# Two plain blocks of a convolutional feed-forward, emitted later behind the sums of h, and each block's taps emitted sequence by sequence

## The chip, the cores and the metric

One core of a Trainium2 chip runs the whole program in one launch. TensorE (PE) multiplies, VectorE (DVE), ScalarE (ACT) and GpSimd (POOL) do the elementwise work, SyncE (SP) issues most of the DMAs, and POOL issues the rest. The metric is the device time of one execution in microseconds (us); a number without a unit below is in us. Times inside an execution count from the start of its span.

## The reference, cut to what matters

Two sequences (256 and 512 tokens, model width 1024) go through two layers. Each layer is a mixer with four branches, which the change does not touch, and then a feed-forward with a depthwise convolution of three taps:

```python
def conv_ffn(h, w_up, w_dw, b_dw, w_down):
    u = depthwise_conv(h @ w_up, w_dw, b_dw)      # over time, per channel, each sequence alone
    a, b = jnp.split(u, 2, axis=-1)               # 2816 channels each
    return (jax.nn.silu(a) * b) @ w_down
...
x = x + conv_ffn(rms_norm(x, ffn_norm[l]), ffn_w_up[l], ffn_conv_w[l], ffn_conv_b[l], ffn_w_down[l])
```

## The kernel before

Both sequences stand side by side as 768 columns, the 512 first. Activations are kept with channels on the 128 partitions. To keep fp32 accuracy each matmul operand is split into a high part (a copy on ACT into fp32r) and a low part (the difference, on DVE), and each product is three matmuls: high x high, low x high, high x low. Weights arrive by DMA (`raw`), ACT makes `whi` (line 444), DVE makes `wlo` (line 453).

**The feed-forward in blocks.** 2816 channels are 22 blocks of 128, numbered 0 to 21. A block is two column groups of `w_up`: the gate half and the value half. Blocks 0 and 1 are *plain*: `ffn_plain` computes each half's 768 columns in two pieces of 384 (`plain_half`, copy out of PSUM by ACT in line 1475). Blocks 2 to 21 are done by `ffn_seven` with seven half-size products instead of eight, in Strassen's manner. For these, sums and differences of the quarters of h are needed. `t_gen` makes them on DVE (lines 640 to 652) with their splits (lines 626 and 628), and `t3_gen` splits one more quarter. The products of a seven-product block stand on PE in this order: `X` (the quarter b11), T1, *T4 of the block before* (`ffn_rest`), T2 (adds into X), b21, b22 and T3 (adds into X again). Each is 12 matmuls of 128x384. ACT copies X after the first product (line 1532), which T2 waits for, because T2 overwrites that PSUM tile. DVE subtracts X after T3 (line 1547), which T4 waits for in the same way. On weights the same scheme needs sums of `raw` tiles, made by DVE (line 435, called `sum`) or by a DMA that accumulates.

**A block's tail** follows its products and is written as generators, resumed at times of the program's own clock:

- for each half `ffn_u`: the middle tap and the bias on ACT (line 1461), then `ffn_conv`, the two outer taps for the 512 columns (lines 1455 and 1457, 128x511) and for the 256 (the same lines, 128x255). All four are DVE operations with both tensors in SBUF
- `ffn_glu`: tanh on ACT (line 1569), a multiply-add on DVE (line 1571), a product of the two halves on POOL (line 1572), the high part on ACT (line 1574), the low part on DVE (line 1576)

After blocks 2 to 4 comes a *down step*, the product of blocks 0 to 3 with `w_down`, into the PSUM tiles `mm`; then blocks 5 to 8 and the down step of 4 to 7, and so on (`FF_SEQ`). So a down step needs the low part of the block that was finished last but one. Its matmuls take the blocks in order, so that part is needed for the fourth block of four.

**What sets the order.** Nothing is scheduled by a tool: every engine runs its instructions in the order in which this program emits them. The program keeps a clock (`self.now`) that advances with each emitted matmul by an estimate of its length. A generator in `self.fast` is resumed when the clock has passed its time; the number that it yields is the delay until the next resumption. `go_fast(gen, delay)` starts one. Weight splits are emitted by `pump` at the same points. So a delay decides only behind which other instructions an operation stands on its engine; the waits themselves are semaphores.

The change touches `ffn_u` (line 1464), which all 22 blocks use, and the two `go_fast` calls of `ffn_plain` (lines 1497 and 1501).

Of the kernel before, what the change touches and what calls it, by code (L numbers as in the profile page):

```python
# [19 lines left out]
NS, NP = 512, 256  # L20
NT = NS + NP
# [226 lines left out]
class Net:  # L248
# [1215 lines left out]
    def ffn_u(self, u, z, col):  # L1464

        self.ffn_mid(u, z, col)
        yield 1.3
        for c0, c1 in ((0, NS), (NS, NT)):
            self.ffn_conv(u, z[:, c0:c1], col, c0, c1)

    def plain_half(self, z, c0, w, rel=0):

# [4 lines left out]
    def ffn_plain(self):  # L1477

        cols = [c + j for j in range(FF_PLAIN) for c in (0, NFF)]
        n = 3  # L1480
        wts = [self.units(2, 128) for _ in cols]
        zs = [self.b() for _ in cols]
        self.finish(0)
        for w, z in zip(wts[:n], zs):
            self.plain_half(z, 0, w)
        self.finish(HALF)
        e = [self.now, self.t_gen()]
        self.fast.append(e)
        for w, z in zip(wts[:n], zs):
            self.plain_half(z, HALF, w, 4)  # L1490
        for w, z in zip(wts[n:], zs[n:]):
            self.plain_half(z, HALF, w)
            if w is wts[-1]:
                self.run_out(e)
                e = [self.now, self.t3_gen()]
                self.fast.append(e)
                self.go_fast(self.ffn_block(0, *zs[0:2]), 1.0)
            self.plain_half(z, 0, w, 4)
        self.run_out(e)
        for j in range(1, FF_PLAIN):  # L1500
            self.go_fast(self.ffn_block(j, *zs[2 * j:2 * j + 2]), 12.0 * j)

    def y(self):
        return self.pm.tile([128, NT], F32, tag="y", name=self.nm("y"), bufs=3)
# [274 lines left out]
```

## Time and profile before

| | |
|---|---|
| runs | 2726.26, 2729.82, 2730.07; median 2729.82 |
| the profiled execution | 2730.13, its span 2728.4 |
| mean granted TensorE clock | 0.989 of full speed |
| PE busy | 2677.2 (98% of the span) |
| DVE busy | 1729.2 (63%) |
| ACT busy | 1141.3 (42%) |
| POOL busy | 634.0 (23%) |
| share of the chain that ended last | PE 86%, DVE 8%, ACT 2%, POOL 1%, DMA 1% |

The profile is of one execution. Busy shares are means over the whole span, and the four engines stand idle at different places. The stretch that the change touches is the feed-forward of each layer. In layer 0 its tails begin at about 880, and five of its down steps begin between 932 and 1314. In layer 1 the same rows come 1358.9 later. A wait is attributed to the semaphore that came last.

### The profile page before, as it was taken

The numbers are of one execution on the slowest core, as the hardware profiler recorded it, in microseconds if no ns is written. First come the engines' busy times: TensorE is split into PE (matmuls) and PEld (weight loads), VectorE is DVE, ScalarE is ACT, GpSimd is POOL, SyncE is SP. The second block draws the span as 40 slices with busy tenths as digits, with TensorE's granted clock in tenths as the row PEclk, the third lists the DMA queues.
The fourth block names the chain that finished last, engine by engine and source line by source line (L and its number), as shares of the span: only waits on it lengthen the run. The fifth ranks groups of instructions, "written<-read, shape, count | busy, mean of one in ns | idle before, by whom it ended". The sixth has DMA issues, their size and how long they took to land.

```text
span 2728.4 us, 40139 instructions
## 1 busy us (share of the span) xinstructions
PE 2677.2 (98%) x15196; PEld 2439.2 (89%) x15196; DVE 1729.2 (63%) x3048; ACT 1141.3 (42%) x2333; POOL 634.0 (23%) x592
## 2 busy tenths in 40 slices
PE   9999999999998999999999999999999989999999
PEld 8779998888898899999987799988888989999998
DVE  6644448887437866686746454478873388766875
ACT  6443443223224554554544434432232255544553
POOL 3402123122222212222314021131121212222221
PEclk9999999999999999999999999999999999999999
DMA  5101113212232466646731111131212325567556
GB/s 167 43 28 37 41 56 114 63 62 62 62 129 81 107 148 128 155 121 147 193 94 43 28 40 48 51 114 63 66 59 62 132 74 127 137 130 161 125 136 163
DMA packets 143264, 258.87 MB, mean 95 GB/s; under 512 B 20192, under 2 KB 36192, under 8 KB 143072
## 3 DMA queue, kind: packets, MB, share of 16 engines
q1 hardware_dynamic: 118368, 197.59, 22.7%
q0 software_dynamic: 24704, 58.73, 12.4%
q8 instruction: 119, 1.95, 0.3%
q14 instruction: 73, 0.60, 0.1%
HBM read 205.78 MB, written 48.91 MB: 93 GB/s over the span
## 4 chain that ended last, share of the span: by engine, by line
PE 86%; DVE 8%; issue 2%; ACT 2%; POOL 1%; DMA 1%; SPq 0%; DVEq 0%; ACTq 0%; POOLq 0%
PE mm L498 35%; PE ps L498 26%; PE mm L522 16%; PE ps L511 3%; DVE wlo L453 2%; PE ps L904 1%; PE ps L1137 1%; PE ps L937 1%; PE ps L1088 1%; DMA raw<-wu 1%; PE ps L1140 1%; POOL st L529 1%; DVE b L612 1%; DVE hl L628 0%; PE ps L851 0%
## 5 line engine op out<-in xcount | busy, mean ns | idle before, releaser
L453 DVE TENSOR_TENSOR wlo<-raw,whi 128x512 fp32r<-128x512 f32 (+1 forms) x616 | 480.8, 790 | 142.3 <-ACT whi L444 117.9
L498 PE MATMUL ps<-b,whi 128*128 128x384 f32 (+2 forms) x1888 | 466.2, 340 | 17.3 <-ACT s L1532 11.7
L444 ACT CAST whi<-raw 128x512 fp32r<-128x512 f32 (+1 forms) x616 | 370.0, 614 | 237.2 <-PE ps L498 72.3
L498 PEld LDWEIGHTS ps<-b,whi 128*128 128x128 f32 x1888 | 329.7, 191 | 34.4 <-ACT s L1532 12.3
L498 PE MATMUL mm<-b,whi 128*128 128x512 f32 (+1 forms) x1504 | 322.9, 336 | 0.6 <-DVE b L1576 0.6
L522 PE MATMUL mm<-whi,hh 128*128 128x512 f32 (+2 forms) x752 | 308.8, 411 | 7.5 <-ACT hh L547 5.7
L498 PE MATMUL mm<-hh,whi 128*128 128x512 f32 (+1 forms) x1152 | 302.1, 343 | 0.0
L498 PE MATMUL ps<-b,wlo 128*128 128x384 f32 (+2 forms) x944 | 299.1, 339 | 0.0
L498 PE MATMUL mm<-hh,wlo 128*128 128x512 f32 (+1 forms) x1152 | 296.8, 338 | 0.0
L498 PE MATMUL mm<-hl,whi 128*128 128x512 f32 (+1 forms) x1152 | 294.7, 337 | 0.0
L522 PE MATMUL mm<-whi,hl 128*128 128x512 f32 (+2 forms) x752 | 278.8, 371 | 0.8 <-DVE hl L554 0.8
L522 PE MATMUL mm<-wlo,hh 128*128 128x512 f32 (+2 forms) x752 | 278.5, 370 | 0.0
L498 PE MATMUL ps<-hh,whi 128*128 128x384 f32 x768 | 259.6, 338 | 8.5 <-ACT whi L444 8.5
L498 PEld LDWEIGHTS mm<-b,whi 128*128 128x128 f32 x1504 | 237.0, 188 | 26.6 <-DVE b L1576 1.2
L498 PE MATMUL ps<-hl,whi 128*128 128x384 f32 x768 | 259.4, 338 | 1.2 <-DVE hl L628 1.2
L498 PE MATMUL ps<-hh,wlo 128*128 128x384 f32 x768 | 258.2, 336 | 0.0
L529 POOL TENSOR_TENSOR st<-st,mhalf 128x16 f32<-128x16 f32 (+5 forms) x50 | 95.0, 1900 | 573.6 <-DVE st L1012 355.7
L1368 POOL TENSOR_TENSOR b<-b,b 128x768 f32<-128x768 f32 x48 | 100.2, 2087 | 463.4 <-DVE b L1363 463.4
L498 PEld LDWEIGHTS mm<-hh,whi 128*128 128x128 f32 x1152 | 177.3, 189 | 26.6 <-issue 3.1
L522 PEld LDWEIGHTS mm<-whi,hh 128*128 128x128 f32 x752 | 177.6, 236 | 25.6 <-issue 10.2
L498 PEld LDWEIGHTS mm<-hl,whi 128*128 128x128 f32 x1152 | 175.7, 188 | 25.1
L498 PEld LDWEIGHTS mm<-hh,wlo 128*128 128x128 f32 x1152 | 176.0, 188 | 24.4
(233 smaller groups left out, 4607.9 us busy)
## 6 DMA issues: line engine op xcount, KB each, us to landing
raw<-wu SPq DMA_DIRECT2D x600, 256.0 KB, 2.7
xsp<-y POOLq DMA_DIRECT2D x66, 384.0 KB, 5.8
raw<-wu POOLq DMA_DIRECT2D x80, 256.0 KB, 4.9
b<-xsp SPq DMA_DIRECT2D x24, 384.0 KB, 6.8
xsp<-b POOLq DMA_DIRECT2D x22, 384.0 KB, 5.7
do<-ot SPq DMA_DIRECT2D x36, 132.0 KB, 1.8
b<-do SPq DMA_DIRECT2D x12, 384.0 KB, 3.5
raw<-wu SPq DMA_DIRECT2D x16, 208.0 KB, 3.6
```

The costliest lines, as they stand in the source:

```text
L444: self.nc.scalar.copy(hi, raw)
L453: self.nc.vector.tensor_sub(lo, raw, hi.bitcast(F32))
L498: nc.tensor.matmul(ap, w, x[:, c0:c1], start=(k == 0 and i == 0 and not more), stop=(k == K - 1 and i == 2), skip_group_check=more)
L511: self.nc.tensor.transpose(out, x, self.ident)
L522: nc.tensor.matmul(ap, x[:, cols], w, start=(k == 0 and i == 0), stop=(k == 7 and i == 2))
L529: self.nc.gpsimd.tensor_tensor(r, ms, self.mhalf[:, 0:n], op=ALU.pow)
L612: nc.vector.scalar_tensor_tensor(h, h, g[:, k:k + 1], self.rbc[:, cols], op0=ALU.mult, op1=ALU.mult)
L904: nc.tensor.matmul(sc[:, 0:S], qkT[hh][:, 128 * t:128 * t + 128], qkT[4 + hh][:, 128 * t0:128 * t0 + S], start=True, stop=True)
L937: nc.tensor.matmul(sh["po"][:, hh, :], PT[:, 128 * kb:128 * kb + 128], v[(t0 + kb) // 3][:, (t0 + kb) % 3, 64 * hh:64 * hh + 64], start=(k ...
L1088: nc.tensor.matmul(sc[:, x, y, 0:W], qT[y][rr, 128 * t:128 * t + 128], kT[y][rr, k0:k0 + W], start=True, stop=True)
L1137: nc.tensor.matmul(po[:, 0, 2 * y + par, :], PT[0:c - a, 2 * z + y, :], vv[:, hc], start=(z == 0), stop=(z == 1))
L1368: nc.gpsimd.tensor_add(a, a, t)
```

## The change

The first conv half of each block now yields 0.9 between the taps of the 512 columns and those of the 256. The tail of block 0 starts 9.0 after the last plain product's first piece instead of 1.0, and that of block 1 starts 18.0 after the plain products instead of 12.0.

```diff
--- before.py
+++ after.py
@@ -1465,8 +1465,9 @@
 
         self.ffn_mid(u, z, col)
         yield 1.3
-        for c0, c1 in ((0, NS), (NS, NT)):
-            self.ffn_conv(u, z[:, c0:c1], col, c0, c1)
+        self.ffn_conv(u, z[:, 0:NS], col, 0, NS)
+        yield 0.9
+        self.ffn_conv(u, z[:, NS:NT], col, NS, NT)
 
     def plain_half(self, z, c0, w, rel=0):
 
@@ -1494,11 +1495,11 @@
                 self.run_out(e)
                 e = [self.now, self.t3_gen()]
                 self.fast.append(e)
-                self.go_fast(self.ffn_block(0, *zs[0:2]), 1.0)
+                self.go_fast(self.ffn_block(0, *zs[0:2]), 9.0)
             self.plain_half(z, 0, w, 4)
         self.run_out(e)
         for j in range(1, FF_PLAIN):
-            self.go_fast(self.ffn_block(j, *zs[2 * j:2 * j + 2]), 12.0 * j)
+            self.go_fast(self.ffn_block(j, *zs[2 * j:2 * j + 2]), 18.0 * j)
 
     def y(self):
         return self.pm.tile([128, NT], F32, tag="y", name=self.nm("y"), bufs=3)
```

All lines from 1469 on move down by one, so line 1532 of before is 1533 of the changed kernel, 1547 is 1548, 1571 is 1572 and 1576 is 1577. The same instructions are emitted on every engine, 3048 on DVE in both; PE's matmuls keep their order. What moves is the order on DVE, ACT and POOL, and with it some DMA issues. Three places on DVE follow (tiles are named by the program; the last number of a name is the program's running number, which shifts between the two).

Place 1 is DVE at the end of the sums of h in layer 0, before. `hl` are low parts of h, `y_..._8231` is the first half of plain block 0, and `sum_..._8275` is a weight sum of block 3:

```order
L628 TENSOR_TENSOR hl_1342_7261<-b_1355_7276,hh_1341_7260 128x384
L1455 SCALAR_TENSOR_TENSOR y_1490_8231<-b_1440_7890,fc_1_80,y_1490_8231 128x511
L1457 SCALAR_TENSOR_TENSOR y_1490_8231<-b_1440_7890,fc_1_80,y_1490_8231 128x511
L1455 SCALAR_TENSOR_TENSOR y_1490_8231<-b_1440_7890,fc_1_80,y_1490_8231 128x255
L1457 SCALAR_TENSOR_TENSOR y_1490_8231<-b_1440_7890,fc_1_80,y_1490_8231 128x255
L453 TENSOR_TENSOR wlo_1492_8252<-raw_1475_8132,whi_1491_8236 128x512
L628 TENSOR_TENSOR hl_1344_7263<-b_1356_7278,hh_1343_7262 128x384
L453 TENSOR_TENSOR wlo_1497_8273<-raw_1437_7866,whi_1493_8261 128x512
L435 TENSOR_TENSOR sum_1498_8275<-raw_1475_8132,raw_1474_8130 128x512
```

and with the change (`y_..._8311` is that half of block 0, `sum_..._8269` that weight sum):

```order
L628 TENSOR_TENSOR hl_1342_7261<-b_1355_7276,hh_1341_7260 128x384
L453 TENSOR_TENSOR wlo_1491_8246<-raw_1475_8132,whi_1490_8234 128x512
L628 TENSOR_TENSOR hl_1344_7263<-b_1356_7278,hh_1343_7262 128x384
L453 TENSOR_TENSOR wlo_1496_8267<-raw_1437_7866,whi_1492_8255 128x512
L435 TENSOR_TENSOR sum_1497_8269<-raw_1475_8132,raw_1474_8130 128x512
L453 TENSOR_TENSOR wlo_1500_8287<-sum_1497_8269,whi_1498_8277 128x512
L435 TENSOR_TENSOR sum_1501_8289<-sum_1497_8269,raw_1476_8134 128x512
L453 TENSOR_TENSOR wlo_1503_8306<-raw_1476_8134,whi_1502_8297 128x512
L453 TENSOR_TENSOR wlo_1507_8326<-sum_1501_8289,whi_1505_8316 128x512
L1455 SCALAR_TENSOR_TENSOR y_1504_8311<-b_1440_7890,fc_1_80,y_1504_8311 128x511
```

The four taps of block 0 stood ahead of two weight splits, a split of h and the weight sum; now they stand behind these and four more weight operations. Their two sequences still follow each other directly.

Place 2 is DVE ahead of the subtraction that T4 of block 3 waits for, before (`s_..._8265` is block 2, `s_..._8399` block 3's value half):

```order
L1571 SCALAR_TENSOR_TENSOR s_1495_8265<-s_1495_8265,s_1520_8397 128x768
L453 TENSOR_TENSOR wlo_1548_8544<-raw_1515_8364,whi_1547_8534 128x512
L1544 TENSOR_TENSOR s_1521_8398<-s_1521_8398,ps_1527_8430 128x384
L453 TENSOR_TENSOR wlo_1551_8557<-raw_1519_8394,whi_1549_8546 128x512
L1547 TENSOR_TENSOR s_1522_8399<-s_1522_8399,ps_1523_8400 128x384
```

and with the change:

```order
L1572 SCALAR_TENSOR_TENSOR s_1494_8259<-s_1494_8259,s_1518_8388 128x768
L453 TENSOR_TENSOR wlo_1549_8548<-raw_1517_8383,whi_1546_8533 128x512
L1455 SCALAR_TENSOR_TENSOR y_1548_8537<-b_1443_7893,fc_1_80,y_1548_8537 128x511
L1457 SCALAR_TENSOR_TENSOR y_1548_8537<-b_1443_7893,fc_1_80,y_1548_8537 128x511
L1455 SCALAR_TENSOR_TENSOR y_1548_8537<-b_1443_7893,fc_1_80,y_1548_8537 128x255
L1457 SCALAR_TENSOR_TENSOR y_1548_8537<-b_1443_7893,fc_1_80,y_1548_8537 128x255
L1548 TENSOR_TENSOR s_1520_8390<-s_1520_8390,ps_1521_8391 128x384
```

The four taps of block 1's second half now stand between block 2's multiply-add and the subtraction; of the two splits and the addition that stood there, one split is left.

Place 3 is DVE ahead of the low part of block 7 (line 1576), which the second down step takes as its last operand, before (`s_..._9479` and `s_..._9480` are block 8):

```order
L1571 SCALAR_TENSOR_TENSOR s_1686_9324<-s_1686_9324,s_1713_9478 128x768
L1544 TENSOR_TENSOR s_1714_9479<-s_1714_9479,ps_1722_9512 128x384
L453 TENSOR_TENSOR wlo_1741_9625<-raw_1710_9458,whi_1740_9615 128x512
L1547 TENSOR_TENSOR s_1715_9480<-s_1715_9480,ps_1716_9481 128x384
L453 TENSOR_TENSOR wlo_1746_9646<-raw_1726_9538,whi_1743_9635 128x512
L1576 SCALAR_TENSOR_TENSOR b_1737_9594<-s_1686_9324,b_1736_9593 128x768
```

and with the change:

```order
L1545 TENSOR_TENSOR s_1714_9479<-s_1714_9479,ps_1722_9509 128x384
L1572 SCALAR_TENSOR_TENSOR s_1686_9324<-s_1686_9324,s_1713_9478 128x768
L453 TENSOR_TENSOR wlo_1741_9625<-raw_1710_9456,whi_1740_9613 128x512
L1548 TENSOR_TENSOR s_1715_9480<-s_1715_9480,ps_1716_9481 128x384
L453 TENSOR_TENSOR wlo_1746_9646<-raw_1726_9538,whi_1743_9635 128x512
L1455 SCALAR_TENSOR_TENSOR s_1744_9638<-s_1714_9479,fc_1_80,s_1744_9638 128x511
L1457 SCALAR_TENSOR_TENSOR s_1744_9638<-s_1714_9479,fc_1_80,s_1744_9638 128x511
L1577 SCALAR_TENSOR_TENSOR b_1739_9605<-s_1686_9324,b_1738_9604 128x768
```

The pair of 128x511 taps of block 8's first half moved ahead of block 7's low part, and the addition of line 1544 (now 1545) ahead of its multiply-add. The same difference stands at the low parts of blocks 11 and 15 and, of block 3, at the first down step. Layer 1 repeats all three places. On ACT, the middle tap of line 1461 for block 8 likewise moved ahead of block 7's high part.

## Rows read from the trace of the kernel before

**Rows 1.** The page, engines' busy time, share of span, instructions.

```profile
PE 2677.2 (98%) x15196; PEld 2439.2 (89%) x15196; DVE 1729.2 (63%) x3048; ACT 1141.3 (42%) x2333; POOL 634.0 (23%) x592
```

**Rows 2.** Waits of PE in the whole span: waiter, awaited, total us, times, longest.

```profile
PE ps L498 <- ACT s L1532: 11.7, 2, 5.9
...
PE ps L498 <- DVE s L1547: 5.4, 3, 2.5
```

**Rows 3.** Timeline of PE, 880 to 938: start, us, instruction, idle before and releaser.

```profile
888.34 1.01 PE L498 MATMUL ps<-b,whi 128*128 128x384 f32 x2 [5.84 <-ACT s L1532]
...
920.08 1.01 PE L498 MATMUL ps<-b,whi 128*128 128x384 f32 x2 [2.49 <-DVE s L1547]
...
935.90 0.62 PE L498 MATMUL mm<-b,whi 128*128 128x512 f32 x2 [0.21 <-DVE b L1576]
```

**Rows 4.** Stretches: length, PE, PEld, DVE, ACT, POOL busy, granted clock, DMA.

```profile
888.00:892.30 4.30, 3.96 (x12) 3.96 (x13) 4.26 (x8) 2.66 (x5) 0.00 (x0) 0.50 0.01 4
...
920.20:924.00 3.80, 3.80 (x14) 3.80 (x15) 3.76 (x6) 2.63 (x6) 0.00 (x0) 0.59 0.42 138
```

**Rows 5.** Timeline of ACT around the first wait, 880 to 888.

```profile
880.02 1.03 ACT L1461 ACTIVATE y<-b,fc 128x768 f32<-128x768 f32 x1
...
887.29 0.62 ACT L444 CAST whi<-sum 128x512 fp32r<-128x512 f32 x1 [3.08 <-DVE sum L435]
887.81 0.47 ACT L1532 COPY s<-ps 128x384 f32<-128x384 f32 x1
```

**Rows 6.** Timeline of DVE, 882 to 935.

```profile
882.00 0.56 DVE L628 TENSOR_TENSOR hl<-b,hh 128x384 fp32r<-128x384 f32 x1 [1.23 <-ACT hh L626]
882.48 0.75 DVE L1455 SCALAR_TENSOR_TENSOR y<-b,fc,y 128x511 f32<-128x511 f32 x1
...
883.93 0.48 DVE L1455 SCALAR_TENSOR_TENSOR y<-b,fc,y 128x255 f32<-128x255 f32 x1
...
884.84 0.68 DVE L453 TENSOR_TENSOR wlo<-raw,whi 128x512 fp32r<-128x512 f32 x1
...
886.52 0.68 DVE L435 TENSOR_TENSOR sum<-raw,raw 128x512 f32<-128x512 f32 x1
...
919.49 0.54 DVE L1547 TENSOR_TENSOR s<-s,ps 128x384 f32<-128x384 f32 x1
...
934.90 0.95 DVE L1576 SCALAR_TENSOR_TENSOR b<-s,b 128x768 fp32r<-128x768 f32 x1
```

**Rows 7.** Timeline of POOL, two products of block tails.

```profile
913.48 1.85 POOL L1572 TENSOR_TENSOR b<-b,y 128x768 f32<-128x768 f32 x1 [14.91 <-DVE b L1571]
916.82 2.19 POOL L1572 TENSOR_TENSOR s<-s,s 128x768 f32<-128x768 f32 x1 [1.50 <-DVE s L1571]
```

**Rows 8.** Timeline of POOL and DVE in the mixer, around 534.

```profile
534.09 2.16 POOL L1368 TENSOR_TENSOR b<-b,b 128x768 f32<-128x768 f32 x1 [8.11 <-DVE b L1363]
...
534.47 2.73 DVE L1241 SCALAR_TENSOR_TENSOR b<-b,mc,b 128x508 f32<-128x508 f32 x2
```

**Rows 9.** Timeline of DVE ahead of the second down step.

```profile
1021.95 0.95 DVE L1571 SCALAR_TENSOR_TENSOR s<-s,s 128x768 f32<-128x768 f32 x1
...
1023.28 2.15 DVE L453 TENSOR_TENSOR wlo<-raw,whi 128x512 fp32r<-128x512 f32 x1
...
1025.82 0.68 DVE L453 TENSOR_TENSOR wlo<-raw,whi 128x512 fp32r<-128x512 f32 x1
1026.43 0.95 DVE L1576 SCALAR_TENSOR_TENSOR b<-s,b 128x768 fp32r<-128x768 f32 x1
```

**Rows 10.** Timeline of ACT there: the high part of block 7.

```profile
1024.92 0.85 ACT L1574 ACTIVATE b<-s 128x768 fp32r<-128x768 f32 x1 [0.20 <-POOL s L1572]
```

**Rows 11.** Timeline of PE in that down step: its fourth block.

```profile
1027.19 0.86 PE L498 MATMUL mm<-b,whi 128*128 128x512 f32 x4
```

**Rows 12.** Timeline of PE in layer 1's mixer: an idle time.

```profile
1478.26 0.32 PE L511 MATMUL ps<-hc,b 128*96 128x128 f32 x1 [1.63 <-DVE b L762]
```

**Rows 13.** The stretch behind that idle time, columns as in rows 4.

```profile
1478.30:1482.00 3.70, 3.70 (x21) 3.07 (x22) 2.95 (x7) 2.00 (x5) 0.21 (x1) 1.00 0.00 0
```

## The prediction

> **What bounds the kernel now.** I read the page's engine table first, then the list of what PE waits for, then PE's own timeline at the three longest of these waits in the feed-forward, the granted clock of the stretch behind them, and last the timelines of the engine that PE was waiting for. PE is busy for 98% of the span [rows 1]. A change that moves no matmul can therefore act only through the little that PE waits, or through waits that it makes. The waits for ACT's copy of X add up to 11.7 in two occurrences, and those for line 1547 to 5.4 [rows 2]. Both come once per layer: 5.84 at 888.34, ahead of T2 of block 2, and 2.49 at 920.08, ahead of T4 of block 3 [rows 3]. A third, 0.21 at 935.90, is the first down step waiting for the low part of block 3.
>
> Behind the two longer waits the granted clock reads 0.50 and 0.59 [rows 4]. Twelve matmuls took 4.00 there instead of 2.08, so the first wait costs 1.92 more than itself. The second stretch costs (1 - 0.59) x 3.80 = 1.58 more.
>
> The chain of the first wait can be read backwards. PE waits for the copy that ACT starts at 887.81; the copy stood on ACT behind `whi<-sum`, which waited 3.08 for DVE's weight sum [rows 5]. DVE started that sum at 886.52, and from 882.48 to 884.84, 2.36 long, it had done the four taps of block 0 [rows 6]. These taps are what the change takes from that place.
>
> From the same rows come the prices that I use, as the time from one start to the next on a DVE that doesn't wait. A 384-column operation is 0.47 (882.00 to 882.48), four taps are 2.36, and the pair of 128x511 taps alone is 1.45 (882.48 to 883.93) [rows 6]. A weight split or sum is 0.60 (1025.82 to 1026.43), and a multiply-add or low part is 0.87, the 1.33 from 1021.95 to 1023.28 less 0.47 [rows 9].
>
> **The change part by part.** *The first wait gets shorter.* Block 0's middle tap, at 880.02 on ACT, costs ACT 0.9 [rows 5] ahead of the split of h that DVE waits 1.23 for [rows 6]. With the change it stands behind, so DVE starts that split at 881.10. Then come 0.47 + 0.60 + 0.47 + 0.60, and the sum starts at 883.24. From sum to `whi` took 0.77, to the copy 0.52, to PE 0.53. T2 starts at 885.06 instead of 888.34: the wait falls from 5.84 to 2.6, and 3.3 are won. The wait that is left is as long as the one of 2.49, so I leave it a clock cost of 1.58, and 0.3 more are won.
>
> *Then DVE is late for T4.* What has moved back still stands ahead of the subtraction of block 3. Before, from 882.00 to the end of that subtraction, 919.95, there are 37.95. Of these 32.2 are work: 18 splits and sums x 0.60, 8 x 0.47, 6 sets of taps x 2.36 and 4 x 0.87. The other 5.75 are waits. With the change the work is 31.3, as one 0.87 of block 1 falls behind the subtraction. If the waits stay at 5.75, the subtraction ends at 881.10 + 31.3 + 5.75 = 918.2. But I replayed the new order with these prices, and waits come in: DVE has caught up with ACT and PE, and waits for two copies of sums (0.8 and 0.9) and for two products of PE (0.7 and 1.0). It waits about 1.8 for ACT elsewhere. Two holds of about 1.4 come on top, which the next paragraph prices. These overlap what was waited for before in part, and the replay gives 7.8 to 8.4 in all, an end at 920.3 to 920.9. PE arrives 3.6 earlier than before, at 914.0, and waits to about 920.5. What the first wait gave is gone.
>
> *The holds.* A weight split that DVE begins inside a POOL product takes 2.15 instead of 0.68 [rows 9]. In the feed-forward of before no tap begins inside such a product, so nothing there shows whether taps are held too. In the mixer two taps that began 0.4 inside a product took 2.73 together [rows 8], some 1.3 more than the like pair of 1.45. With the change the taps of block 1's second half begin inside the product of block 1 or 2 (the tail's parts move, and these taps now stand ahead of T4's subtraction), so I charge 1.2 to 1.5. A product is 1.85 to 2.19 long [rows 7]. The Trainium skill, "SBUF — State Buffer", section "Who interferes with whom", has a rule for this: a DVE instruction with two SBUF inputs contends with a GpSimd instruction that reads SBUF, and whichever was issued first keeps the shared port for its whole length. The rows in the mixer agree, and by the rule moved taps would be held wherever they meet a product; without it the sum below would be some 1.5 less per layer, 2749 in all.
>
> *The first down step is late.* From the end of T4's subtraction to the start of block 3's low part there were 14.95 [rows 6], of which 13.54 are work. Now there are 15.86: the 0.87 of block 1 and the pair of taps of 1.45 that moved ahead of the low part come in. The wait of 1.42 in it grows to between 3.5 and 4.2, since block 1's high part, waiting for POOL, stands ahead of a middle tap on ACT, and two more holds come in. Then the low part ends at 920.3 + 15.86 + 3.5 + 0.95 = 940.6 at the least, and at 920.9 + 15.86 + 4.2 + 0.95 = 941.9 at the most, instead of 935.85: 4.8 to 6.0 later. I take 6.0, since the products there follow a DVE subtraction as the one of 2.19 does [rows 7]. The lower bound, no wait beyond those of before, is 918.2 + 15.86 + 1.42 + 0.95 = 936.4, or 0.5 later. PE's new wait of about 5 lies between the two that cost clock: 1.6, with bounds 0 and 1.92.
>
> *The later down steps.* At the second one the low part of block 7 starts at 1026.43 and so ends at 1027.38 [rows 9]. PE needs it for the third matmul of the group of four that starts at 1027.19 [rows 11], half of 0.7 in, at 1027.54. The slack is under 0.2. With the change the addition of 0.47 stands ahead of the multiply-add, so the product, which ended just before 1024.92 [rows 10], ends at 1025.4 to 1025.8. The split held by it ends 0.6 later, the pair of taps takes 1.45 and the low part 0.95, which gives 1028.4 to 1028.8. PE waits 0.9 to 1.3, and I take 1.1. The bounds are 0.5, if nothing is held, and 1.75, if 0.47 and 1.45 are simply added to 1027.38. Blocks 11 and 15 have the same order. Of the clock I charge nothing here: after an idle time of 1.63 in layer 1's mixer [rows 12] the granted clock still read 1.00 [rows 13].
>
> *All else.* The other moved rows (the 0.9 between the taps of every other half, the moved DMA issues) I cost at nothing, since PE waits for none of their results and DVE stands idle for 37% of the span; without that cover a set of taps would cost its 2.36.
>
> The sum per layer is 6.0 + 1.6 + 3 x 1.1 = 10.9. The shorter first wait is no term of its own, as PE meets DVE again at T4. Two layers give 21.8. The profiled execution took 2730.13, 0.3 above the median of the runs, so the forecast is **2752**.
>
> **The rivals.** *Faster (chance 0.13).* The first wait shrinks by 3.3 and T4's wait goes with its slow clock. That is 3.3 + 0.3 + 2.49 + 1.58 = 7.7 per layer, and the time is 2715. It decides by whether the subtraction of block 3 ends by 914.0; my replay has it 6 later, the most lenient sum 4 later. For it speaks only that the two longest waits stand exactly there and that DVE idles much on the mean.
>
> *No change (0.12), 2730.* The first wait shrinks, T4 gives it back, and the low parts stay within half a microsecond of now because ACT and POOL run ahead of my replay. A change that doesn't do what it says would land here too, but the order shows its rows moved. Against it stands the slack of under 0.2.
>
> *Only the later down steps are late (0.15).* The first down step absorbs its delay, as in the lower bound, and only the 3 x 1.1 per layer stay: 2736.7.
>
> *Forecast case (0.60).* All three: from 2 x (0.5 + 0 + 1.5) = 4 more, 2734, to 2 x (6.0 + 1.92 + 5.25) = 26 more, 2757.
>
> **How the numbers follow.** A measurement of this kernel can tell some 0.2%, or 5.5, from no change. Slower by more than that hold the forecast case and the third rival, 0.60 + 0.15 = 0.75; within it the second, 0.12; faster the first, 0.13. The range reaches from the rival of no change, 2729, to the top of the forecast case, 2757, and leaves out the faster case. The forecast case's own range is 2734 to 2757.
>
> **What would show it.** In the changed profile the wait ahead of T2 of block 2 should be about 2.6, T4 of block 3 should still wait until about 920.5, and the first down step should wait some 5 for line 1577, with a granted clock of 0.5 to 0.6 behind it. Waits for that line should come eight times in all, six of them of about 1.1. Sets of taps that begin inside a product should read longer than 1.45 a pair. I am wrong if T4 starts before 916, if the low part of block 3 ends before 937, or if the later down steps run without a wait.

## The result and the profile after

| | before | changed |
|---|---|---|
| median of 4 runs each | 2729.57 | 2750.22 |
| lowest and highest | 2726.26, 2730.07 | 2749.23, 2754.10 |
| the profiled execution | 2730.13, span 2728.4 | 2754.10, span 2752.3 |
| mean granted clock | 0.989 | 0.987 |

The changed kernel is slower: the ratio estimated over the runs is 1.0084, with a 95% interval from 1.0071 to 1.0097 (the two medians alone give 1.0076). The forecast was 2752. The profiled execution is the slowest of the four; its parts therefore add up to somewhat more than the medians' difference of 20.7.

The page's engine table of the changed kernel, columns as in [rows 1]:

```profile
PE 2684.6 (98%) x15196; PEld 2443.3 (89%) x15196; DVE 1728.3 (63%) x3048; ACT 1136.7 (41%) x2333; POOL 641.0 (23%) x592
```

DVE has as much work as before. PE has 7.4 more, for the same 15196 matmuls; the stretches with a granted clock of 0.50 and 0.55 below show where it is slower. The waits of PE, with columns as in [rows 2]:

```profile
PE ps L498 <- DVE s L1548: 10.3, 2, 5.1
PE mm L498 <- DVE b L1577: 10.0, 8, 1.4
...
PE ps L498 <- ACT s L1533: 5.2, 2, 2.6
PE mm L498 <- ACT b L1575: 5.1, 2, 2.6
```

The wait for the copy of X is down from 11.7 to 5.2 in the two layers. In its place stand 10.3 for the subtraction of line 1548, 10.0 in eight waits for low parts (line 1577) and 5.1 for high parts (line 1575). PE's timeline shows where they are in layer 0 (against [rows 3]):

```profile
885.74 0.61 PE L498 MATMUL ps<-b,whi 128*128 128x384 f32 x2 [2.58 <-ACT s L1533]
...
909.15 0.45 PE L498 MATMUL ps<-hh,whi 128*128 128x384 f32 x1 [0.74 <-ACT s L1539]
...
914.25 0.61 PE L498 MATMUL ps<-b,whi 128*128 128x384 f32 x2 [0.66 <-DVE s L1542]
...
921.76 1.01 PE L498 MATMUL ps<-b,whi 128*128 128x384 f32 x2 [5.13 <-DVE s L1548]
...
940.66 0.64 PE L498 MATMUL mm<-b,whi 128*128 128x512 f32 x2 [2.49 <-ACT b L1575]
...
942.65 1.01 PE L498 MATMUL mm<-b,whi 128*128 128x512 f32 x2 [1.36 <-DVE b L1577]
...
1038.69 0.62 PE L498 MATMUL mm<-b,whi 128*128 128x512 f32 x2 [1.23 <-DVE b L1577]
```

T2 of block 2 starts at 885.74 after 2.58, T4 of block 3 at 921.76 after 5.13. Then the first down step waits twice, 2.49 for the high part of block 3 and 1.36 for its low part, and the second one waits 1.23. The granted clock behind the waits at T4, at the first down step and at the second one (columns as in [rows 4]):

```profile
921.70:926.50 4.80, 4.74 (x15) 4.74 (x16) 4.73 (x9) 2.48 (x5) 0.00 (x0) 0.50 0.17 55
940.60:945.50 4.90, 3.48 (x11) 2.95 (x12) 4.74 (x8) 1.32 (x3) 0.06 (x1) 0.55 0.34 54
1038.60:1041.00 2.40, 2.31 (x13) 2.22 (x14) 2.27 (x6) 0.80 (x1) 0.19 (x1) 1.00 0.37 69
```

It reads 0.50, 0.55 and 1.00. DVE ahead of T4 and of the low part of block 3 (against [rows 6]), and the two POOL products that the first two of its rows meet:

```profile
902.22 2.33 DVE L435 TENSOR_TENSOR sum<-raw,raw 128x512 f32<-128x512 f32 x1
...
917.25 2.29 DVE L1455 SCALAR_TENSOR_TENSOR y<-b,fc,y 128x511 f32<-128x511 f32 x1
...
921.16 0.55 DVE L1548 TENSOR_TENSOR s<-s,ps 128x384 f32<-128x384 f32 x1
...
931.14 0.75 DVE L1455 SCALAR_TENSOR_TENSOR s<-s,fc,s 128x511 f32<-128x511 f32 x1 [1.28 <-ACT s L1461]
...
941.65 0.95 DVE L1577 SCALAR_TENSOR_TENSOR b<-s,b 128x768 fp32r<-128x768 f32 x1
```

```profile
901.85 2.15 POOL L1573 TENSOR_TENSOR b<-b,y 128x768 f32<-128x768 f32 x1 [5.38 <-DVE b L1572]
...
916.81 2.18 POOL L1573 TENSOR_TENSOR s<-s,s 128x768 f32<-128x768 f32 x1 [12.81 <-DVE s L1572]
```

The sum at 902.22 began inside the product of 901.85 and took 2.33 instead of 0.68; the first tap of block 1's second half began inside the product of 916.81 and took 2.29 instead of 0.75 [rows 6]. The subtraction that T4 waits for could start only at 921.16. At 931.14 stands the wait of 1.28 for the middle tap on ACT, and the low part of block 3 starts at 941.65 instead of 934.90. Ahead of the second down step (against [rows 9]):

```profile
1034.02 0.55 DVE L1548 TENSOR_TENSOR s<-s,ps 128x384 f32<-128x384 f32 x1
...
1034.49 1.82 DVE L453 TENSOR_TENSOR wlo<-raw,whi 128x512 fp32r<-128x512 f32 x1
...
1036.24 0.74 DVE L1455 SCALAR_TENSOR_TENSOR s<-s,fc,s 128x511 f32<-128x511 f32 x1
...
1037.01 0.75 DVE L1457 SCALAR_TENSOR_TENSOR s<-s,fc,s 128x511 f32<-128x511 f32 x1
...
1037.68 0.95 DVE L1577 SCALAR_TENSOR_TENSOR b<-s,b 128x768 fp32r<-128x768 f32 x1
```

```profile
1033.62 2.16 POOL L1573 TENSOR_TENSOR s<-s,s 128x768 f32<-128x768 f32 x1 [1.93 <-DVE s L1572]
```

The split that began inside the product took 1.82 (the subtraction ahead of it, which reads PSUM, only 0.55), the pair of taps follows, and the low part of block 7 stands behind both.

Since PE runs the same matmuls in the same order, the start of one matmul can be compared in the two traces. The difference tells what each place cost (changed minus before):

| matmul | before | changed | difference |
|---|---|---|---|
| last one ahead of T2 of block 2 | 882.15 | 882.83 | 0.67 |
| first of T2 of block 2 | 888.34 | 885.74 | -2.60 |
| first of T4 of block 3 | 920.08 | 921.76 | 1.68 |
| first down step, low part of block 3 | 935.90 | 942.65 | 6.75 |
| last ahead of block 7's low part | 1027.42 | 1037.17 | 9.75 |
| on block 7's low part | 1027.54 | 1038.69 | 11.15 |
| on block 11's low part | 1119.06 | 1131.76 | 12.70 |
| on block 15's low part | 1210.60 | 1224.79 | 14.19 |
| end of the feed-forward of layer 0 | 1329.63 | 1343.26 | 13.63 |

From 0.67 to 13.63 is 12.96 for layer 0. Layer 1's feed-forward goes from 10.51 to 23.97, 13.46. Between the two feed-forwards, where the change does nothing, the difference falls from 13.63 to 10.51. In layer 1's mixer, from 2028 to 2140 alone, it falls by 1.9, with a granted clock of 1.00 in both executions. I take no account of that, and below I compare kernels by these sums over the two feed-forwards, beside their times.

### The profile page after: what moved, and what is told of

Read it like the earlier page. It is cut to its first block, busy times and chain, and to the rows that moved or that the text cites. A ratio compares the mean times of both kernels' runs of the same rounds, so it can differ in the third digit from the quotient of the medians.

```text
span 2752.3 us, 40171 instructions
## 1 busy us (share of the span) xinstructions
PE 2684.6 (98%) x15196; PEld 2443.3 (89%) x15196; DVE 1728.3 (63%) x3048; ACT 1136.7 (41%) x2333; POOL 641.0 (23%) x592
## 4 chain that ended last, share of the span: by engine, by line
PE 84%; DVE 9%; issue 2%; ACT 2%; POOL 1%; DMA 1%; SPq 0%; ACTq 0%; DVEq 0%; POOLq 0%
PE mm L498 34%; PE ps L498 26%; PE mm L522 15%; PE ps L511 3%; DVE wlo L453 3%; PE ps L904 1%; PE ps L1137 1%; PE ps L1088 1%; PE ps L937 1%; DVE s L1455 1%; PE ps L1140 1%; DVE b L1577 1%; POOL st L529 1%; DVE b L612 1%; PE ps L851 0%
## 5 line engine op out<-in xcount | busy, mean ns | idle before, releaser
L453 DVE TENSOR_TENSOR wlo<-raw,whi 128x512 fp32r<-128x512 f32 (+1 forms) x616 | 474.6, 777 | 153.5 <-ACT whi L444 123.3
L498 PE MATMUL ps<-b,whi 128*128 128x384 f32 (+2 forms) x1888 | 469.9, 342 | 16.8 <-DVE s L1548 10.3
L498 PEld LDWEIGHTS ps<-b,whi 128*128 128x128 f32 x1888 | 332.2, 192 | 34.2 <-DVE s L1548 10.9
```

What stands on the lines that cost most here:

```text
L453: self.nc.vector.tensor_sub(lo, raw, hi.bitcast(F32))
L498: nc.tensor.matmul(ap, w, x[:, c0:c1], start=(k == 0 and i == 0 and not more), stop=(k == K - 1 and i == 2), skip_group_check=more)
```

## The experiments

All kernels were timed against the kernel before, each group beside runs of its own of it, whose medians lie between 2727.4 and 2729.6; the ratios carry 95% intervals. "Feed-forwards" is the sum described above, from the profiled executions, for layer 0 and layer 1.

| kernel | median | ratio | feed-forwards |
|---|---|---|---|
| changed | 2750.22 | 1.0084 [1.0071, 1.0097] | 13.0, 13.5 |
| the 0.9 alone | 2746.79 | 1.0075 [1.0060, 1.0090] | 8.3, 11.0 |
| both delays alone | 2733.45 | 1.0025 [1.0015, 1.0034] | 2.6, 3.7 |
| block 0's delay alone | 2733.01 | 1.0020 [1.0009, 1.0031] | 1.1, 2.5 |
| block 1's delay alone | 2735.73 | 1.0033 [1.0021, 1.0046] | 2.6, 5.1 |
| taps apart, tail on time | 2740.26 | 1.0048 [1.0033, 1.0063] | 4.9, 7.4 |
| taps together, tail late | 2762.43 | 1.0127 [1.0112, 1.0142] | 16.2, 17.5 |
| down step behind block 5 | 2730.24 | 1.0013 [1.0004, 1.0023] | |
| that, with 9.0 and 24.0 | 2729.57 | 1.0008 [0.9998, 1.0018] | |
| changed, products on DVE | 2744.39 | 1.0055 [1.0040, 1.0070] | 8.5, 8.6 |
| before, products on DVE | 2724.82 | 0.9988 [0.9979, 0.9998] | |
| block 0's delay, products on DVE | 2726.13 | 0.9990 [0.9981, 1.0000] | |
| down step behind block 5, 9.0 and 24.0, products on DVE | 2726.00 | 0.9985 [0.9976, 0.9994] | |

**The parts of the change, each alone.** The section on the change says that the first half of each block yields the 0.9. Both halves do, since both run `ffn_u`. In blocks 2 to 21 each half is a generator of its own, and only the second half's 0.9 makes the tail's end later. In the plain blocks 0 and 1 both halves and the end are one generator: their second half comes 0.9 later on the program's clock, and their end 1.8.

First the 0.9 without the delays:

```diff
-        for c0, c1 in ((0, NS), (NS, NT)):
-            self.ffn_conv(u, z[:, c0:c1], col, c0, c1)
+        self.ffn_conv(u, z[:, 0:NS], col, 0, NS)
+        yield 0.9
+        self.ffn_conv(u, z[:, NS:NT], col, NS, NT)
```

> The kernel before with the 0.9 between the taps of the two sequences alone; the delays stay 1.0 and 12.0. My theory: the low parts that the first four down steps wait for lose their slack because a pair of 1.45 moved ahead of them, whatever the delays; so the wait for T2 of block 2 stays at 5.8 and that for T4 of block 3 at about 2.5, each of four down steps per layer waits 1.2 to 1.5 and costs 1.5, and the time is 2 x 4 x 1.5 = 12 above the kernel before, about 2741. Rival: the taps apart are harmless and the later waits come from the late tails of blocks 0 and 1; then the time is 2730 and no wait for line 1577 is over 0.5.

PE's timeline at T2 of block 2, T4 of block 3 and the second down step:

```profile
887.07 1.01 PE L498 MATMUL ps<-b,whi 128*128 128x384 f32 x2 [6.77 <-ACT s L1533]
...
919.91 1.01 PE L498 MATMUL ps<-b,whi 128*128 128x384 f32 x2 [3.13 <-DVE s L1548]
...
1031.14 0.61 PE L498 MATMUL mm<-b,whi 128*128 128x512 f32 x2 [1.23 <-DVE b L1577]
```

The waits at the later down steps came as expected, 1.23, with T2 and T4 not relieved. The time is 19.2 above that of before beside it, where 12 was expected: I had not seen that this edit also makes the wait for T2 longer (6.77 against 5.84) and that for T4 (3.13 against 2.49), and that the first down step waits for the high part too. The rival, 2730, is out.

Then both delays without the 0.9:

```diff
-                self.go_fast(self.ffn_block(0, *zs[0:2]), 1.0)
+                self.go_fast(self.ffn_block(0, *zs[0:2]), 9.0)
...
-            self.go_fast(self.ffn_block(j, *zs[2 * j:2 * j + 2]), 12.0 * j)
+            self.go_fast(self.ffn_block(j, *zs[2 * j:2 * j + 2]), 18.0 * j)
```

> The kernel before with the two delays (9.0 and 18.0) alone, the taps of both sequences together. My theory: the wait for T2 of block 2 falls to 2.6; four taps still stand ahead of the subtraction of block 3, so T4 waits 4 to 5; the low part of block 3 comes some 4 later than before (14.4 of work behind that subtraction instead of 15.9), with a slow clock behind it; the later down steps do not wait. 5 to 6 per layer, about 2741. Rival: the delays alone are a gain, and only the yield costs; then 2722 or less.

```profile
885.36 0.61 PE L498 MATMUL ps<-b,whi 128*128 128x384 f32 x2 [2.58 <-ACT s L1532]
...
920.76 1.01 PE L498 MATMUL ps<-b,whi 128*128 128x384 f32 x2 [4.70 <-DVE s L1547]
...
939.02 0.62 PE L498 MATMUL mm<-b,whi 128*128 128x512 f32 x2 [0.99 <-DVE b L1576]
```

The waits are where the theory put them, at T2 2.58 and at T4 4.70, and the first down step waits 0.99 with none later (in layer 1 it also waits 1.53 for the high part). The price was overestimated: 5.9 instead of 11, since the matmul on the low part of block 3 came only 2.8 later (939.02 against 935.90, less the 0.3 by which this execution was late already), without a slow clock behind it. The rival, by which the delays alone are a gain, is out: they cost 0.25%. The two parts add up roughly: 8.3 + 2.6 = 10.9 and 11.0 + 3.7 = 14.7, against the 13.0 and 13.5 of the whole change. So most of the loss is the yield's, though the diff of the delays looks larger.

The delay of block 0 alone (the first of the two lines), and that of block 1 alone (the second):

> The kernel before with the delay of block 0's tail alone (9.0). My theory: DVE has the same 32.2 of work ahead of the subtraction of block 3 and the same 13.5 behind it, so the 3.3 that T2 of block 2 wins (wait 2.6) are waited again at T4 (wait 5 to 6), and the time stays within 0.2% of the kernel before, 2727 to 2731. Rival: the work ahead of T4 was not the bound, and the win stays: 2 x 3.6 less, 2722.

> The kernel before with the delay of block 1's tail alone (18.0). My theory: the wait for T2 stays at 5.8; the four taps of block 1's second half now stand ahead of the subtraction of block 3, and its multiply-add and low part ahead of the low part of block 3, so this delay carries nearly all of what the two delays cost: T4 waits 2 to 4, the first down step 3 to 4, and the time is 2738 to 2742. Rival: the cost comes from block 0's delay, which crowds the queue behind the sums; then 2730.

PE with block 0's delay alone:

```profile
883.62 0.74 PE L498 MATMUL ps<-b,whi 128*128 128x384 f32 x2 [2.58 <-ACT s L1532]
...
908.48 0.45 PE L498 MATMUL ps<-hh,whi 128*128 128x384 f32 x1 [2.20 <-ACT s L1538]
...
919.73 1.01 PE L498 MATMUL ps<-b,whi 128*128 128x384 f32 x2 [3.79 <-DVE s L1547]
```

This is the trade in its plainest form. T2's wait falls to 2.58; then PE waits 2.20 for ACT's copy (line 1538), 0.64 for an addition (line 1541), and 3.79 at T4, which starts at 919.73, 0.35 earlier than before, by an execution that was 1.46 ahead. What T2 won is waited again, and a bit more; at 2733.0 the time is 2 above the range of my expectation, and 5.4 above that of before beside it. Block 1's delay alone keeps T2's wait at 5.86, and the first down step waits 0.99 for its low part (in layer 1 also 2.82 for the high part); 2735.7 is 2 less than I expected, but the rival's 2730 is out. Each delay costs. Block 1's cost more in these runs, though the two intervals overlap, and the costs do not add: with both delays the feed-forwards lose 2.6 and 3.7, no more than with block 1's alone (2.6 and 5.1).

**Taps apart, or the tail late?** The 0.9 does two things: it parts the taps, and everything that a tail emits behind them comes later on the program's clock. One kernel parts the taps and takes 0.9 back in `ffn_last`; one keeps them together and adds 0.9 there. `ffn_last` makes the tails of blocks 2 to 21. So in the first kernel blocks 0 and 1, whose tails are made by `ffn_block`, stay as late as the 0.9 makes them:

```diff
# taps apart, tail on time (beside the yield of 0.9)
         yield from self.ffn_u(u2, z2, NFF + j)
-        yield 2.0
+        yield 1.1
# taps together, tail late (in the kernel before)
-        yield 2.0
+        yield 2.9
```

> The kernel before with the 0.9 between the taps, but with the 2.0 that the tail of a block yields behind its second half's taps cut to 1.1, so that everything behind the taps is emitted when it was before. The taps stay apart; the low parts stand ahead of the next block's taps again. My theory: what cost was not the taps apart but the 0.9 by which the tail's end came later on the program's clock, behind the next block's taps; the four down steps' waits for line 1577 fall to 0.5 or less and the time is 2728 to 2733. Rival: taps apart cost by themselves, as more operations change places among weight splits; then the waits of 1.2 stay and the time is near 2747, that of the 0.9 alone.

> The kernel before with the taps of both sequences together and that same 2.0 raised to 2.9, so that the tail's end comes 0.9 later without any taps apart. All four taps of the next block then stand ahead of a low part. My theory: each of four down steps per layer waits 1.23 + 0.9 = 2.1, at a cost of 2.4 each, 2 x 4 x 2.4 = 19, about 2747, as slow as the 0.9 between the taps or slower. Rival: lateness does not matter and the taps apart do; then 2728 to 2731.

With the tail on time no down step waits for a low part any more (no wait of PE for line 1577 is left in the list of its waits). With the taps together and the tail late each of them waits, 2.14 at the second one:

```profile
1031.71 0.61 PE L498 MATMUL mm<-b,whi 128*128 128x512 f32 x2 [2.14 <-DVE b L1576]
```

```profile
1031.70:1035.00 3.30, 3.29 (x13) 3.21 (x14) 1.85 (x3) 1.42 (x2) 0.87 (x1) 0.69 0.02 5
1035.00:1038.00 3.00, 3.00 (x15) 2.75 (x15) 0.88 (x2) 1.74 (x3) 0.00 (x0) 0.77 0.89 131
```

So the waits of the later down steps come from the 0.9 of lateness, which puts a low part behind taps of the next block; parting the taps is not needed for them. That was my theory, and the size of the wait, 2.1, was right. The time was not: 35 above that of before instead of 19, because behind the wait of 2.14 the granted clock falls to 0.69 and 0.77 in the next two stretches, and the matmul that waits comes 2.31 later while those behind it lose another 2.3 by the next down step (the difference to before is 4.17 there, and 6.44 ahead of the next low part). Behind the 1.23 of the changed kernel it stayed at 1.00.

But the first of the two kernels is still 12.9 slower than before, against my expectation. In layer 0 it loses 0.9 at T2, 2.4 at T4 and 1.9 in the last blocks, where three short waits stand (0.51, 0.91 and 0.41) and before had one of 0.46:

```profile
884.90 1.01 PE L498 MATMUL ps<-b,whi 128*128 128x384 f32 x2 [6.76 <-ACT s L1533]
...
918.46 1.01 PE L498 MATMUL ps<-b,whi 128*128 128x384 f32 x2 [4.92 <-DVE s L1548]
...
1315.88 0.62 PE L498 MATMUL ps<-b,whi 128*128 128x384 f32 x2 [0.91 <-DVE s L1548]
```

ACT ahead of the first of these waits, three weight splits on DVE ahead of the second, and the product of block 1 on POOL:

```profile
882.93 0.62 ACT L444 CAST whi<-sum 128x512 fp32r<-128x512 f32 x1 [4.01 <-DVE sum L435]
...
883.46 1.02 ACT L1461 ACTIVATE y<-b,fc 128x768 f32<-128x768 f32 x1
...
884.39 0.45 ACT L1533 COPY s<-ps 128x384 f32<-128x384 f32 x1
```

```profile
893.24 1.73 DVE L453 TENSOR_TENSOR wlo<-raw,whi 128x512 fp32r<-128x512 f32 x1
...
912.46 2.18 DVE L453 TENSOR_TENSOR wlo<-raw,whi 128x512 fp32r<-128x512 f32 x1 [0.28 <-ACT whi L444]
...
915.90 2.04 DVE L453 TENSOR_TENSOR wlo<-raw,whi 128x512 fp32r<-128x512 f32 x1
```

```profile
915.59 1.80 POOL L1573 TENSOR_TENSOR b<-b,y 128x768 f32<-128x768 f32 x1 [1.50 <-DVE b L1572]
```

On ACT the middle tap of block 0's second half (1.02) has moved between the `whi<-sum` and the copy of X that T2 waits for; before it had run at 883.17, while ACT waited for the sum. That is the 0.9 by which T2 waits longer, and it is lateness: block 0's own first half yields the 0.9 ahead of that tap. On DVE three splits begin inside products and take 1.73, 2.18 and 2.04; before there were two such, of 2.10 and 1.83, ahead of the same subtraction. T4's wait is 4.92 instead of 2.49. The first and the third of these splits meet the products of blocks 0 and 1; the one of 915.59 now comes behind block 2's, where before it came ahead of it (913.48 and 916.82 in [rows 7]). So at T2 and T4 the late plain tails have a part in the loss, and this kernel doesn't show that parted taps cost by themselves; no run here leaves out that lateness. The rival, 2747, was right that the time would not be that of before, and wrongly kept the waits of 1.2.

**What holds DVE.** If POOL's products are what stretches DVE's operations, giving them to DVE itself should pay although it adds 0.9 per block:

```diff
-        nc.gpsimd.tensor_mul(t, t, b)
+        nc.vector.tensor_mul(t, t, b)
```

> The changed kernel with the product of each block's tail done by DVE instead of POOL, at the same place of the program. My theory: what held DVE's operations at 2.3 (a sum, a tap) and 1.8 to 2.9 (splits) is POOL's product. Ahead of the subtraction of block 3 two products add 2 x 0.87 = 1.7 and two holds of 1.6 go; behind it two products add 1.7 and holds of 1.6 and 1.1 and part of a wait of 1.3 go. T4's wait falls to some 3.6, and the low part of block 3 comes 2.5 to 3.5 earlier; each later down step's wait falls by 0.3, to 0.9. 3.3 to 4.3 less per layer: 2741 to 2744. Rival: these lengths are not the product's doing; then DVE is later by 1.7 at T4, 3.5 at the first down step and 0.9 at each later one, and the time is 2760 or more.

The sum, the product of block 2 and the first tap behind it on DVE, and PE at T4 and at the second down step:

```profile
899.94 0.68 DVE L435 TENSOR_TENSOR sum<-raw,raw 128x512 f32<-128x512 f32 x1
...
912.83 0.96 DVE L1573 TENSOR_TENSOR s<-s,s 128x768 f32<-128x768 f32 x1
...
914.31 0.74 DVE L1455 SCALAR_TENSOR_TENSOR y<-b,fc,y 128x511 f32<-128x511 f32 x1
```

```profile
917.27 1.01 PE L498 MATMUL ps<-b,whi 128*128 128x384 f32 x2 [4.59 <-DVE s L1548]
...
1031.68 0.61 PE L498 MATMUL mm<-b,whi 128*128 128x512 f32 x2 [1.03 <-DVE b L1577]
```

The sum takes 0.68 and the tap 0.74 where they took 2.33 and 2.29; the product takes 0.96. From the start of T2 to that of the subtraction it is 34.17 instead of 35.42, 1.25 less (1.5 expected), and to the low part of block 3 53.19 instead of 55.91, 2.7 less. T4's wait shrinks by only 0.54, to 4.59 instead of the 3.6 expected, as PE comes earlier too: its wait of 0.74 for a copy is gone. The later down steps wait 1.03. The time, 2744.4, is 0.4 above the 2741 to 2744 expected; the rival's 2760 is out. That the holds are gone is read from these lengths; the product's result also comes sooner than from POOL (0.96 instead of 2.2), and the time doesn't tell the two gains apart. The Trainium skill, "SBUF — State Buffer", section "Who interferes with whom", has the rule that a DVE instruction with two SBUF inputs and a GpSimd instruction that reads SBUF exclude each other for their whole length. The traces agree on the side of DVE: in the changed kernel all 36 DVE operations with both tensors in SBUF that begin inside one of the 44 products (2 taps, 2 sums, 32 splits) end 0.54 to 0.56 after it.

The same edit was made to the kernel before and to that with block 0's delay:

> The kernel before with the products on DVE. My theory: three products add 2.6 ahead of the subtraction of block 3, and the two holds there (1.4 and 1.15) go, so T4's wait stays near 2.5; behind it 0.9 comes in and a hold of about 1.4 goes. 2726 to 2731, no change. Rival: DVE has less room than that and the 19 us of products per layer come through, 2740 or more.

> The kernel with block 0's tail at 9.0 alone, and the products on DVE. My theory: T2 keeps its wait of 2.6; the waits for ACT's copy (2.2) and at T4 (3.8) fall by what the holds cost above the products' 0.87, so this beats the 2733 of block 0's delay alone by 2 to 6, 2727 to 2731. Rival: three products ahead of T4 weigh more than the holds that go; then 2735 or more.

Both came out 1 below the range expected, 0.12% and 0.10% below the kernel before, the second with an interval that reaches 1.0000. The kernel before with the products on DVE, on its page:

```profile
PE 2670.9 (98%) x15196; PEld 2435.6 (89%) x15196; DVE 1724.9 (63%) x3092; ACT 1142.9 (42%) x2333; POOL 548.2 (20%) x548
```

DVE does 44 operations more and is busy for 1724.9 instead of 1729.2 [rows 1]: the time that its operations stood held, which counts as busy, was more than the 44 products take on DVE.

**Taking the due time away.** The first down step was moved behind block 5, and then the two tails were delayed further:

```diff
-("u", 4), ("d", 0, 4), ("u", 5), ("u", 6)
+("u", 4), ("u", 5), ("d", 0, 4), ("u", 6)
# second kernel, in addition: delays 9.0 and 24.0
```

> The kernel before with its first down step moved behind block 5, its weights packed and loaded in that order; delays 1.0 and 12.0. This takes the first down step's due time away from DVE. My theory: the waits for T2 (5.8) and T4 of block 3 (2.5 to 3.7, as two splits more stand ahead) stay, the low part of block 3 is early, and the time is that of before, 2727 to 2733. Rival: the moved down step finds its weights late or a buffer occupied; then a new wait and 2735 or more.

> As the kernel with the first down step behind block 5, with block 0's tail at 9.0 and block 1's at 24.0. The work of DVE ahead of the subtraction of block 3 falls from 32.2 to 27.8. My theory says that work is the bound there, so T2's wait falls to 2.6 and T4's is 0 to 3 instead of growing to 5, the down step has a block's time for its low parts, and the time is 2715 to 2723, faster than both kernels. Rival: the delayed parts come back as waits of the next block's products (T2, T4 of block 4 or 5) and the time stays at 2727 or more.

The move alone is 0.13% slower, with waits of 5.87 at T2 and 3.69 at T4; that is as expected. PE in the second kernel, at T4 of block 3, behind the next block's T1, and at T4 of block 4:

```profile
916.81 1.01 PE L498 MATMUL ps<-b,whi 128*128 128x384 f32 x2 [2.31 <-DVE s L1547]
...
928.71 0.45 PE L498 MATMUL ps<-hh,whi 128*128 128x384 f32 x1 [1.75 <-ACT s L1538]
...
937.50 1.01 PE L498 MATMUL ps<-b,whi 128*128 128x384 f32 x2 [2.27 <-DVE s L1547]
```

T2 waits 2.59 and T4 of block 3 2.31, about as expected. But 1.75 for the copy of line 1538 and 2.27 at T4 of block 4 are new. That is the rival: what was put off comes back a block later. The time, 2729.6, is not the 2715 to 2723 of my theory, and cannot be told from that of before.

With the products on DVE in addition:

> The kernel with the first down step behind block 5 and the tails of blocks 0 and 1 at 9.0 and 24.0, and the products on DVE. My theory: without holds the waits of 2.3 (T4 of block 3), 1.75 (copy) and 2.3 (T4 of block 4) shrink by about 1 each, and the time is 2721 to 2727, faster than both kernels by 0.1 to 0.3%. Rival: the later blocks lack the room on DVE, 2732 or more.

The waits at T4 of block 3 and of block 4 shrink to 1.59 and 1.30, as the theory had it, but that for the copy grows from 1.75 to 3.28. 2726.0 is within what was expected, and 0.15% below the kernel before, with an interval that ends at 0.9994. No version is faster than before by more than 0.2%. That of before with the products on DVE is as fast with a single word changed.

## Why the prediction was right

- **The first wait.** It was forecast at 2.6 and measured 2.58, with the sum, the `whi` and the copy where the replay had them (883.24 for the sum, against 883.92 in an execution that was 0.67 late before).
- **T4 takes it back.** T4 was to wait until about 920.5; it waited until 921.76, in an execution that was 0.67 late before. PE arrived later than the 914.0 forecast, as it had two waits on the way that the replay lacks (0.74 and 0.66), so the wait was 5.13 and not 6.5; the time of the start is what counts. That DVE's work ahead of the subtraction sets it is shown by block 0's delay alone (the win is waited again) and by the later delays (27.8 of work by the expectation there, T4's wait 2.31 though T2 came as early).
- **The holds.** Charged at 1.2 to 1.5, the tap's was 1.55 (2.29 against 0.74), at the place named. With the products on DVE they are gone.
- **The first down step.** The low part's matmul was to be 6.0 later; it is 6.75 - 0.67 = 6.08 later. PE's wait for it is 2.49 + 1.36, in two parts and not some 5 for line 1577, since PE came later and the high part was late as well.
- **Its clock cost** was mis-sized: 1.6 forecast, 3.0 measured, beyond even the upper bound of 1.92. From 6.75 to 9.75 the matmuls behind it lost 3.0. In layer 1 it is 2.3, beyond that bound too. I had priced one slow stretch behind one wait; here two waits in a row, 2.49 and 1.36, stand ahead of it. That this is the reason is not shown: behind two in a row of 1.00 and 1.38, with the 0.9 alone, nothing was lost in layer 0.
- **The later down steps** were to wait 1.1 each and waited 1.23; each cost 1.4. The step from wait to cost was taken as one to one.
- **The sum.** 6.08 + 3.0 + 3 x 1.4, with small changes behind, is 12.96 for layer 0, against 10.9 forecast. The total of the profiled execution is 24.0, of the medians 20.7, against 21.8. So the total was nearer than its terms, and that is luck: the two undersized terms make 4 to 5 in the two layers, and the executions of the changed kernel differ by as much (2749.23 to 2754.10).
- **All else** was costed at nothing. As a sum that holds for the changed kernel: 6.08 + 3.0 + 3 x 1.4 is 0.3 more than the 12.96. As a statement on the yield it doesn't: the 0.9 alone also made the waits at T2 and T4 longer, by 0.93 and 0.64 in layer 0 (T2's part of that is not in the changed kernel, whose wait there is 2.58). And the delays, on which I rested T4 and most of the first down step, cost 5.9 alone. The replay of the whole order was right; which edit makes what share of it I had not worked out, and my expectations for the parts missed by 2 to 15, in both directions.
- **Two slips in the working** change nothing in the forecast. (1 - 0.59) x 3.80 is 1.56, not 1.58. And the 5.75 called waits ahead of T4's subtraction hold some 2.6 of holds, of the two splits that took 2.10 and 1.83; so the kernel before had two holds there already, and those of the changed kernel come in place of them.

What stays open is why PE's same matmuls in layer 1's mixer take 1.9 less in some executions than in others at the same granted clock, why the kernel with the taps apart and the tail on time loses less in layer 0 (4.9) than in layer 1 (7.4), and how much of that loss is the parting and how much the late tails of blocks 0 and 1; no run tells these apart.

## What to carry to other kernels

Where an engine works through its queue in the order of the program, an operation that is put off is still ahead of somebody: add up the work that stands between the last point where the engine was free and each due time, before and after, and see which due time has no slack. A yield inside a generator moves everything that comes behind it, not only the operations on its two sides, once for each time that the generator runs it; look for the consumer at the tail's end first. And price an operation by what runs beside it: the same tap took 0.74 or 2.29, and the product that held it costs 0.96 on the held engine itself.

## What the runs showed of the hardware

- Behind a wait of 1.23 the granted clock stayed at 1.00; behind one of 2.14 it read 0.69 and 0.77 in the next stretches, and the matmuls there lost 2.3 more. Behind the 5.13 of T4 it read 0.50 over the next 4.8.
- A DVE operation that begins inside a POOL product is held to its end if both its tensors lie in SBUF: a sum (2.33), a tap (2.29), a split (1.73 to 2.18). The subtraction at 1034.02, with one operand in PSUM, began inside the product of 1033.62 and took 0.55; so did all 28 such subtractions of the changed kernel (0.54 to 0.56).
- The holds cost DVE more than the products would: with the 44 products on DVE instead of POOL its busy time fell from 1729.2 to 1724.9.
- The same product of 128x768 takes 0.96 on DVE and, in the changed kernel, 1.83 to 2.23 on POOL.
